# Transposing the third group's attention weights on VectorE, and scattering the merge statistics earlier

## The chip, the cores and the metric

The kernel runs on one core of one Trainium2 chip. The metric is the device time of one execution in microseconds (us). A core has TensorE (PE in the profile, with its weight loads as PEld), VectorE (DVE), ScalarE (ACT), GpSimd (POOL) and SyncE (SP), each with a queue of its own; DMAs are issued from the queues of SP, POOL and ACT.

## The reference

Two decoder layers on 512 tokens of 1024 channels: a mixer, then a SwiGLU FFN with 2816 hidden channels, with an RMSNorm ahead of each and one at the end. The change lies in the first layer's mixer, a mixture of three dilated causal attentions with ALiBi, and in the last step of the first FFN.

```python
ATTN_PAIRS = ((128, 1), (512, 4), (2048, 16))        # (window, dilation) of the three groups, 8 heads of 128 each
...
# group g: query t attends to keys t - j*dil, j = 0..window/dil
s = jnp.einsum('bnqhd,bnkhd->bnhqk', qb, kb) * (D ** -0.5) + bias
p = jnp.exp(s - m); den = jnp.sum(p, axis=-1, keepdims=True)
o = jnp.einsum('bnhqk,bnkhd->bnqhd', p / den, vb)
lse = (m + jnp.log(den))[..., 0]
...
wts = jax.nn.softmax(jnp.stack(lses, axis=0), axis=0)  # over the three groups
o = jnp.sum(wts[..., None] * o, axis=0)
return o.astype(h.dtype) @ w_out
```

So the three groups of one head are one softmax over all their keys: each group contributes a maximum and a sum for each query, and these are merged.

## The kernel before

**Numbers.** Every large product is made in fp32 precision from three fp32r matmuls: an operand is split into a high and a low part (`split`, L77 on ACT and L78 on DVE), and hi x hi, hi x lo and lo x hi are added up in PSUM. Weights arrive by DMA in a ring of raw tiles and are split into a ring of five `whi`/`wlo` pairs, some products ahead of their use (`pump`).

**Products.** Plain products (`Product.add`, L254 to L257) run over 512 columns. From the second head on, two 128-column weight blocks at a time go through `seven`, which makes a 2x2 block product with seven half-size ones (L371 to L373, 12 matmuls of 256 columns each, about 1.44 us) and adds on DVE (L412, L418/L420, L425, L426). It holds four PSUM banks, `p1`, `p26`, `p45` and `p73`, of the eight in the ring `ps()`; a new bank is one that was taken eight allocations before. `values12` (L483 to L485) is the same thing for the values of groups 2 and 3. Between the products, `behind(i)` calls other work that is due there: a dictionary `after` maps the place to functions, and `between(h, g)` writes it for head h's three q/k pairs (g = 0, 1, 2). The tile framework then orders each engine's instructions from that program.

**Token order.** Tokens are stored by residue mod 4 (`r`), so that each residue's 128 tokens (`i`) are one block for groups 2 (dilation 4) and 3 (dilation 16). Group 1 needs them by blocks of 128 neighbours: `by_block` and `in_a_row` are the views that change from one order to the other. At the end of the first FFN `unfold` (L879) puts all tokens in natural order for the pooling layer.

**A head's attention**, one head behind the projections:

- `scores0` and `scores12` make the scores of group 1 (`s0`) and of groups 2 and 3 (`s12`, 128 queries x 4 residues x 2 groups x 128 keys), their maxima on DVE and the exponentials with their sums on ACT (L577, L601). Maxima and sums are kept in `st`: `st[:, 0]` for both orders of queries, a column for each block or residue.
- `merge` brings group 1's statistics to the order of groups 2 and 3 and the other way round. For this it spreads each statistic over four columns, of which `place` leaves one (partition mod 4) non-zero (`far`, L614), multiplies by `swap` on PE (L618; ones where two partitions lie in the same group of four), and picks out and adds up (L621, L624). From both it makes the factors `co`, and scales `s0` on DVE (L633) and `s12` on ACT (L636).
- `turn0` and `turn12` transpose the weights on PE, 128x128 at a time with `ident` (L645, L656), and ACT copies them out of PSUM (L646, L657). `turn_values` (L540) does so for group 1's values.
- `output` multiplies values and transposed weights (L669 to L672, L678).

`far` lies in the buffer of `b12`, the bias tile of `scores12`. A list `mark` holds the last DVE subtraction of each `seven` or `values12`, and `merge` issues `far` behind the latest of them.

Of the kernel before, what the change touches and what calls it, by code (L numbers as in the profile page):

```python
# [2 lines left out]

# [12 lines left out]
P = 128  # L16
S = 512
# [31 lines left out]
def trunk(ctx: ExitStack, tc: tile.TileContext, xT, norms, w_first, w_qk, w_qkp, w_v0, w_v0p, w_v12, w_out, w_pair, w_down, w_pin, w_pgrp,  # L49
# [304 lines left out]

        return t.rearrange("p (a c) -> p a c", a=2)


    mark = []

    def by_block(t, a=slice(0, 2)):  # L360

        return t.rearrange("p (b i r) -> p r i b", b=NT, r=NT)[:, 2 * a.start:2 * a.stop]
# [17 lines left out]
    def seven(T, one, two, scratch, after={}, blocks=False):  # L380


        unit, = units.popleft()
        into, left, right = by_block if blocks else in_place, slice(0, 1), slice(1, 2)

        def again(v):
            return v.unsqueeze(1).to_broadcast([P, 2, H2])

        p1, p26, p45, p73 = ps(), ps(), ps(), ps()

        def behind(i):
# [12 lines left out]
        w = part(unit, "s")  # L404
        mult(p45[:, H2:], w, 0, T, "1")
        behind(2)
        mult(p73[:, :H2], w, 1, T, "3")
        w.done()
        behind(3)
        w = part(unit, "m")  # L410
        mult(p26[:, H2:], w, 0, T, "2")
        nc.vector.tensor_add(into(one), p26, again(first[:, :H2]))  # L412
        behind(4)
        mult(p73[:, H2:], w, 1, T, "22")
        w.done()
        if blocks:
            for a in (left, right):
                nc.vector.tensor_add(in_place(sums, a), in_place(p73, a), into(one, right))  # L418
        else:
            nc.vector.tensor_add(sums, p73, again(one[:, H2:]))  # L420
        behind(5)
        w = part(unit, "l")
        mult(p45[:, :H2], w, 0, T, "4")
        w.done()
        nc.vector.tensor_sub(into(two), p45, again(sums[:, :H2]))  # L425
        mark.append(nc.vector.tensor_sub(into(one, right), sums[:, H2:], p45[:, H2:]))  # L426
        behind(6)

    def normed(layer, k, row):
# [21 lines left out]
    with tc.tile_pool(name="opool", bufs=1) as opool:  # L451
        early = opool.tile([P, HEADS, S], F32R, tag="o", name="early")
        with tc.tile_pool(name="apool", bufs=1) as apool:
# [15 lines left out]
            def values12(after={}):  # L469


                t = apool.tile([P, NT, 4 * P], F32, name="v12")
                unit = units.popleft()

                def product(name, half, key):
                    p = ps()
                    for a in range(2):
                        for k in range(K2):
                            wh, wl = (v[:, half * S + k % 2 * H2:half * S + (k % 2 + 1) * H2]
                                      for v in part(unit[k // 2], name).t)  # L480
# [47 lines left out]
                mark.append(nc.vector.tensor_sub(quarter(0, 1), both(m4), both(u3)))  # L528
                behind(6)
                return t  # L530

# [49 lines left out]
            def scores12(h):  # L581
# [19 lines left out]
                    nc.scalar.activation(v, v, AF.Exp, bias=nm[:, 1, r:r + 1], accum_out=st[:, 0, 1, 1, r:r + 1])  # L601
                A[h]["s12"] = s12

            def merge(h):


                st, s0, s12 = A[h]["st"], A[h]["s0"], A[h]["s12"]
                mx = apool.tile([P, 2, NT], F32, name="mx")
                ex = apool.tile([P, 2, 2, NT], F32, name="ex")
                dd = apool.tile([P, 2, 2, NT], F32, name="dd")  # L610
                co = apool.tile([P, 2, NT], F32, name="co")
                far = apool.tile([P, 4 * NT, NT], F32, tag="b12", name="far")
                with tc.issue_after(mark[-1].ins) if mark else nullcontext():
                    nc.vector.tensor_mul(far, st[:, 0].rearrange("p a s b -> p (a s b)").unsqueeze(2).to_broadcast(  # L614
                        [P, 4 * NT, NT]), place[:, None].to_broadcast([P, 4 * NT, NT]))
                p = ps()
                for a in range(2):
                    nc.tensor.matmul(p[:, a * 32:(a + 1) * 32], swap,  # L618
                                     far[:, (1 - a) * 8:(2 - a) * 8].rearrange("p s r -> p (s r)"), start=True, stop=True)

                nc.vector.tensor_mul(far.rearrange("p (q r) b -> p q r b", r=NT),  # L621
                                     p[:, :64].rearrange("p (q b r) -> p q r b", b=NT, r=NT),
# [26 lines left out]
            def turn12(h):  # L649

                s12 = A[h]["s12"]
                t12 = apool.tile([P, NT, 2, P], F32, name="t12")
                for half in range(2):
                    p = ps()
                    for a in range(4):
                        nc.tensor.transpose(blk(p, a), s12[:, 2 * half + a // 2, a % 2, :], ident)  # L656
                    nc.scalar.copy(t12[:, 2 * half:2 * half + 2].rearrange("p a g k -> p (a g k)"), p)  # L657
                A[h]["t12"] = t12

            def output(h):  # L660
# [15 lines left out]
                for r in range(NT):  # L676
                    for g in (1, 2):
                        nc.tensor.matmul(blk(po, r), blk(QKV[h // 2, 12, 2][:, r, :], h % 2 * 2 + g - 1),  # L678
                                         t12[:, r, g - 1, :],
                                         start=g == 1, stop=g == 2)  # L680
                nc.vector.tensor_add(o0, o0, po)

# [81 lines left out]
            def between(h, g):  # L764

                if g == 0:
                    return {2: [later(merge, h - 1)], 4: [later(turn_values, h - 1)] if h > 1 else []} if h % 2 else {
                        1: [later(output, h - 2)], 2: [later(merge, h - 1)]}
                if g == (2 if h == 1 else 1):
                    return {0: [later(turn0, h - 1)], 2: [later(turn12, h - 1)], 4: [later(scores0, h)]}  # L770
# [17 lines left out]
                prepare(2 + c)  # L788
            scores12(0)
            turn_values(0)  # L790
            for h in range(1, HEADS):
                for g in range(3):
                    if h == 1 and g < NSOLO:
# [17 lines left out]
                        nc.gpsimd.dma_start(X[k], xT[:, k, :])  # L811
                if h % 2 == 0:
                    VT[:] = [apool.tile([P, S], F32, tag=tag, name="vt") for tag in ("row", "o0")]
                    seven(T, *VT, scratch, {0: [later(scores12, h)]}, True)
                elif h < HEADS - 1:
                    QKV[h // 2, 12, 2] = values12({0: [later(scores12, h)]})
                else:
                    QKV[h // 2, 12, 2] = values12({0: [later(scores12, h)], 1: [later(halve, 0), later(halve, 1)],
                                                   2: [later(halve, 2), later(halve, 3)], 3: [later(merge, h)],
                                                   4: [later(halve, 4), later(halve, 5)]})  # L820
            for k in range(KC):
                give(("h", k))
# [29 lines left out]
    with tc.tile_pool(name="fpool", bufs=2) as fpool:  # L852
# [19 lines left out]
        def unfold(m, p):  # L872
# [3 lines left out]
                new = t[:, 0]  # L876
            else:
                new = x_tile(m - 1)
            nc.vector.tensor_add(new.rearrange("p (b i r) -> p r i b", r=NT, b=NT), *(  # L879
                t.rearrange("p (r i b) -> p r i b", r=NT, b=NT) for t in (X[m], p)))  # L880
            X[m] = new

        def ffn(layer, nxt, lead, row):
# [281 lines left out]
```

## Time and profile before

| | |
|---|---|
| runs of the kernel | 1268.6, 1269.49 and 1269.86 us, median 1269.49 |
| profiled execution | 1268.85 us, span from first to last instruction 1267.0 us |
| granted TensorE clock over the span | 0.998 |
| PE busy | 1252.6 us, 8310 instructions |
| DVE busy | 919.1 us, 1383 instructions |
| ACT busy | 566.7 us, 879 instructions |
| attention, first to last head | from the start to about 463 us |
| first FFN | about 510 to 858 us |

A row of the timeline gives start and length in us, engine, line, operation, tiles written and read (buffer numbers left out), shape, how many were merged into the row, and in brackets how long the engine had been idle and what ended that. A row of the groups gives the number of instructions, their joint busy time in us, the mean length of one in ns, and the idle time ahead of them. A row of the waits gives who waited for whom, the total in us, how often, and the longest. PE's records overlap, so the time that a PE instruction takes on its engine is the distance to the next start. An fp32 matmul that isn't split is two records; a transpose is one.

### The profile page before, as it was taken

How to read it: one execution, taken by the hardware profiler on the slowest of the kernel's cores; microseconds unless marked ns; L12 is line 12 of the kernel's file. 1: busy time of each engine (PE TensorE's matmuls, PEld its weight loads, DVE VectorE, ACT ScalarE, POOL GpSimd, SP SyncE). 2: the span in 40 equal slices, each digit the busy share in tenths (PEclk: the TensorE clock that was granted, in tenths of full speed). 3: DMA queues.
4: the chain of work that ended last, by engine and by line, in shares of the span. 5: the costliest groups of instructions: out<-in, count | busy, mean ns of one | idle time of the engine just before them, and what ended most of it. 6: DMA issues, size and time to landing. Idle time of an engine off the chain costs nothing.

```text
span 1267.0 us, 20887 instructions
## 1 busy us (share of the span) xinstructions
PE 1252.6 (99%) x8310; PEld 1154.3 (91%) x8310; DVE 919.1 (73%) x1383; ACT 566.7 (45%) x879; POOL 127.0 (10%) x121
## 2 busy tenths in 40 slices
PE   9999999999999999999999999999999999999997
PEld 7889999999999988889989999888788988999987
DVE  6987788878778845778636887558977853788643
ACT  6445554545445543444424554343444532455331
POOL 2011111211111000001001110000300000111000
PEclk9999999999999999999999999999999999999999
DMA  8336566655756433247457774334124745677322
GB/s 290 105 93 166 132 156 146 159 141 144 180 139 152 138 136 115 67 96 178 131 140 166 182 186 126 99 130 132 38 78 107 173 131 138 171 183 172 93 69 67
DMA packets 67330, 172.45 MB, mean 136 GB/s; under 512 B 6928, under 2 KB 9120, under 8 KB 67232
## 3 DMA queue, kind: packets, MB, share of 16 engines
q1 hardware_dynamic: 48816, 135.97, 34.3%
q0 software_dynamic: 17264, 34.09, 16.1%
q8 instruction: 65, 1.06, 0.3%
q10 hardware_dynamic: 1152, 1.05, 0.2%
q14 instruction: 33, 0.27, 0.1%
HBM read 168.99 MB, written 2.10 MB: 135 GB/s over the span
## 4 chain that ended last, share of the span: by engine, by line
PE 74%; issue 12%; DVE 9%; DMA 2%; ACT 1%; POOL 1%; DVEq 0%; POOLq 0%
PE ps L372 12%; PE ps L371 12%; PE ps L373 12%; PE ps L255 8%; PE ps L254 8%; PE ps L257 8%; DMA raw<-w_pair 2%; PE ps L483 2%; PE ps L484 2%; PE ps L485 2%; DVE wlo L78 2%; PE ps L678 1%; PE ps L590 1%; DVE raw L434 1%; POOL rcol L323 1%
## 5 line engine op out<-in xcount | busy, mean ns | idle before, releaser
L77 ACT ACTIVATE whi<-raw 128x1024 fp32r<-128x1024 f32 (+2 forms) x297 | 295.3, 1000 | 438.4 <-PE ps L255 196.5
L78 DVE TENSOR_TENSOR wlo<-raw,whi 128x1024 fp32r<-128x1024 f32 (+2 forms) x297 | 340.4, 1150 | 150.2 <-ACT whi L77 149.1
L254 PE MATMUL ps<-a,whi 128*128 128x512 f32 (+1 forms) x374 | 141.0, 377 | 0.0
L255 PE MATMUL ps<-a,whi 128*128 128x512 f32 (+1 forms) x374 | 140.9, 377 | 0.0
L257 PE MATMUL ps<-a,wlo 128*128 128x512 f32 (+1 forms) x374 | 140.8, 377 | 0.0
L371 PE MATMUL ps<-tt,whi 128*128 128x256 f32 x384 | 108.7, 283 | 0.0
L372 PE MATMUL ps<-tt,whi 128*128 128x256 f32 x384 | 108.7, 283 | 0.0
L373 PE MATMUL ps<-tt,wlo 128*128 128x256 f32 x384 | 108.7, 283 | 0.0
L137 POOL DMA_DIRECT2D raw<-w_pair x32 | 38.7, 1210 | 446.2 <-DMA raw<-w_pair 158.8
L257 PEld LDWEIGHTS ps<-a,wlo 128*128 128x128 f32 x374 | 70.4, 188 | 13.0
L254 PEld LDWEIGHTS ps<-a,whi 128*128 128x128 f32 x374 | 70.4, 188 | 12.8
L255 PEld LDWEIGHTS ps<-a,whi 128*128 128x128 f32 x374 | 70.4, 188 | 12.7
L371 PEld LDWEIGHTS ps<-tt,whi 128*128 128x128 f32 x384 | 73.7, 192 | 0.0
L372 PEld LDWEIGHTS ps<-tt,whi 128*128 128x128 f32 x384 | 73.7, 192 | 0.0
L373 PEld LDWEIGHTS ps<-tt,wlo 128*128 128x128 f32 x384 | 73.7, 192 | 0.0
L372 PE MATMUL ps<-tb,whi 128*128 128x256 f32 x256 | 72.6, 284 | 0.9 <-DVE tb L78 0.9
L371 PE MATMUL ps<-h,whi 128*128 128x256 f32 x252 | 72.7, 289 | 0.0
L373 PE MATMUL ps<-tb,wlo 128*128 128x256 f32 x256 | 72.4, 283 | 0.0
L371 PE MATMUL ps<-tb,whi 128*128 128x256 f32 x256 | 72.4, 283 | 0.0
L373 PE MATMUL ps<-h,wlo 128*128 128x256 f32 x252 | 71.3, 283 | 0.0
L372 PE MATMUL ps<-h,whi 128*128 128x256 f32 x252 | 71.3, 283 | 0.0
L254 PE MATMUL ps<-h,whi 128*128 128x512 f32 x160 | 62.7, 392 | 0.0
(280 smaller groups left out, 3420.3 us busy)
## 6 DMA issues: line engine op xcount, KB each, us to landing
raw<-w_pair SPq DMA_DIRECT2D x76, 512.0 KB, 4.5
raw<-w_qkp SPq DMA_DIRECT2D x36, 512.0 KB, 4.5
raw<-w_pair POOLq DMA_DIRECT2D x32, 512.0 KB, 7.3
raw<-w_down SPq DMA_DIRECT2D x32, 384.0 KB, 3.1
raw<-w_down SPq DMA_DIRECT2D x32, 320.0 KB, 2.9
raw<-w_v SPq DMA_DIRECT2D x18, 512.0 KB, 4.1
raw<-w_qkp POOLq DMA_DIRECT2D x18, 512.0 KB, 7.2
rawhalf<-w_pair SPq DMA_DIRECT2D x32, 256.0 KB, 3.5
```

Source lines behind the costliest of these rows:

```text
L77: nc.scalar.activation(hi, v, AF.Copy)
L78: nc.vector.tensor_tensor(lo, v, hi.bitcast(F32), op=OP.subtract)
L137: nc.gpsimd.dma_start(self.b.t.rearrange("p (a c) -> p a c", a=2), self.src[:, None, 3 * S:].to_broadcast([P, 2, S]), accum_op=OP.add)
L254: nc.tensor.matmul(self.p[:, cols], w[0][:, s], mh[:, cols], start=self.done == 0, stop=False)
L255: nc.tensor.matmul(self.p[:, cols], w[0][:, s], ml[:, cols], start=False, stop=False)
L257: nc.tensor.matmul(self.p[:, cols], w[1][:, s], mh[:, cols], start=False, stop=self.done == self.n)
L371: nc.tensor.matmul(dst, w.t[0][:, c], th, start=k == 0, stop=False)
L372: nc.tensor.matmul(dst, w.t[0][:, c], tl, start=False, stop=False)
L373: nc.tensor.matmul(dst, w.t[1][:, c], th, start=False, stop=k == K2 - 1)
L483: nc.tensor.matmul(o, mh, wh, start=k == 0, stop=False)
L484: nc.tensor.matmul(o, mh, wl, start=False, stop=False)
L485: nc.tensor.matmul(o, ml, wh, start=False, stop=k == K2 - 1)
```

## The change

**Transposes.** Within each residue the tokens are put in another order (`turned`): the 128 tokens of a residue mod 4 are now four runs of 32, one for each residue mod 16. In group 3 a query attends only to keys of its own residue mod 16, so its 128x128 weights are zero outside the four 32x32 blocks on the diagonal. `turn12` now transposes group 2's four blocks on PE as before, and group 3's with one `nc.vector.transpose` from SBUF to SBUF, which transposes each 32x32 block in place. `t12` is laid out by group first. Masks and the input's order are prepared to match on the host.

**Merge.** A new function `scatter` makes `far` with the two halves of the statistics exchanged, so that one matmul of 64 columns replaces two of 32. It is called in the value stage of the head itself and no longer in `merge` during the next head's first q/k pair, and the list `mark` is gone. For odd heads `merge` and `turn_values` are called one product earlier (at 1 and 3 in place of 2 and 4).

**Unfold.** The new order can't be undone by one view of four dimensions, so the add that ends the first FFN is made in four parts of 128 columns, with both inputs strided and the output contiguous.

```diff
             def merge(h):
-                far = apool.tile([P, 4 * NT, NT], F32, tag="b12", name="far")
-                with tc.issue_after(mark[-1].ins) if mark else nullcontext():
-                    nc.vector.tensor_mul(far, st[:, 0].rearrange("p a s b -> p (a s b)").unsqueeze(2).to_broadcast(
-                        [P, 4 * NT, NT]), place[:, None].to_broadcast([P, 4 * NT, NT]))
                 p = ps()
-                for a in range(2):
-                    nc.tensor.matmul(p[:, a * 32:(a + 1) * 32], swap,
-                                     far[:, (1 - a) * 8:(2 - a) * 8].rearrange("p s r -> p (s r)"), start=True, stop=True)
+                nc.tensor.matmul(p[:, :64], swap, far.rearrange("p s r -> p (s r)"), start=True, stop=True)
...
+            def scatter(h):
+                far = apool.tile([P, 2, 2 * NT, NT], F32, tag="b12", name="far")
+                nc.vector.tensor_mul(far, A[h]["st"][:, 0, ::-1].rearrange("p a s b -> p a (s b)").unsqueeze(3)
+                                     .to_broadcast([P, 2, 2 * NT, NT]), place[:, None, None].to_broadcast([P, 2, 2 * NT, NT]))
+                A[h]["far"] = far.rearrange("p a s r -> p (a s) r")
...
             def turn12(h):
                 s12 = A[h]["s12"]
-                t12 = apool.tile([P, NT, 2, P], F32, name="t12")
-                for half in range(2):
-                    p = ps()
-                    for a in range(4):
-                        nc.tensor.transpose(blk(p, a), s12[:, 2 * half + a // 2, a % 2, :], ident)
-                    nc.scalar.copy(t12[:, 2 * half:2 * half + 2].rearrange("p a g k -> p (a g k)"), p)
+                t12 = apool.tile([P, 2, NT, P], F32, name="t12")
+                p = ps()
+                for r in range(NT):
+                    nc.tensor.transpose(blk(p, r), s12[:, r, 0, :], ident)
+                nc.scalar.copy(t12[:, 0].rearrange("p r k -> p (r k)"), p)
+                nc.vector.transpose(t12[:, 1], s12[:, :, 1, :])
...
-                    return {2: [later(merge, h - 1)], 4: [later(turn_values, h - 1)] if h > 1 else []} if h % 2 else {
+                    return {1: [later(merge, h - 1)], 3: [later(turn_values, h - 1)] if h > 1 else []} if h % 2 else {
                         1: [later(output, h - 2)], 2: [later(merge, h - 1)]}
...
+            scatter(0)
...
-                    seven(T, *VT, scratch, {0: [later(scores12, h)]}, True)
+                    seven(T, *VT, scratch, {0: [later(scores12, h)], 4: [later(scatter, h)]}, True)
...
-                    QKV[h // 2, 12, 2] = values12({0: [later(scores12, h)]})
+                    QKV[h // 2, 12, 2] = values12({0: [later(scores12, h)], 4: [later(scatter, h)]})
...
         def unfold(m, p):
-            nc.vector.tensor_add(new.rearrange("p (b i r) -> p r i b", r=NT, b=NT), *(
-                t.rearrange("p (r i b) -> p r i b", r=NT, b=NT) for t in (X[m], p)))
+            for b in range(NT):
+                nc.vector.tensor_add(new[:, b * P:(b + 1) * P], *(
+                    t.rearrange("p (r j i b) -> p b i j r", r=NT, j=NT, b=NT)[:, b] for t in (X[m], p)))
```

In the last head `scatter` and `merge` both stand in the value stage, at 2 and 3.

How the rows move is shown at head 3's first q/k pair, where head 2 is merged. A number behind a name is that of the buffer; lines of the new kernel are a few lower than the old ones (L620 was L621, L412 is L409). On PE, the second product of `seven` (before `ps_1794`, now `ps_1784`), the third (`ps_1795`, now `ps_1785`) and the exchange; before:

```order
L371 MATMUL ps_1795<-tx_590,whi_1631 128x256
L372 MATMUL ps_1795<-tx_591,whi_1631 128x256
L373 MATMUL ps_1795<-tx_590,wlo_1632 128x256
L371 MATMUL ps_1794<-t_387,whi_1703 128x256
L618 MATMUL ps_1852<-far_1850,const_90 128x32 x2
L371 MATMUL ps_1796<-t_390,whi_1631 128x256
```

And now:

```order
L368 MATMUL ps_1784<-h_587,whi_1589 128x256
L369 MATMUL ps_1784<-h_587,whi_1589 128x256
L370 MATMUL ps_1784<-h_587,wlo_1590 128x256
L618 MATMUL ps_1824<-far_1747,const_90 128x64
L368 MATMUL ps_1785<-t_387,whi_1619 128x256
L369 MATMUL ps_1785<-t_387,whi_1619 128x256
```

The exchange stood behind the third product and one matmul of the fifth; it now stands right behind the second, 13 matmuls earlier, and is one matmul.

On DVE at the same place (`vt` are head 2's values, `raw`, `halflo` and `wlo` the weights of later products), before:

```order
L426 TENSOR_TENSOR vt_1649<-sums_1668,ps_1653 128x2x32x4
L150 TENSOR_TENSOR raw_1594<-raw_1594,raw_1595 128x512
L78 TENSOR_TENSOR halflo_1843<-rawhalf_1596,halfhi_1842 128x512
L151 TENSOR_TENSOR raw_1594<-raw_1594 128x512
L614 TENSOR_TENSOR far_1850<-st_1459,place_457 128x64
L621 TENSOR_TENSOR far_1850<-ps_1852,place_457 128x64
```

And now, from five rows earlier on:

```order
L409 TENSOR_TENSOR vt_1637<-ps_1640,first_1655 128x4x32x4
L606 TENSOR_TENSOR far_1747<-st_1447,place_457 128x64
L78 TENSOR_TENSOR wlo_1731<-raw_1582,whi_1730 128x1024
L415 TENSOR_TENSOR sums_1656<-ps_1642,vt_1637 128x256 x2
L78 TENSOR_TENSOR wlo_1764<-raw_1583,whi_1763 128x1024
L422 TENSOR_TENSOR vt_1638<-ps_1641,sums_1656 128x4x32x4
L423 TENSOR_TENSOR vt_1637<-sums_1656,ps_1641 128x2x32x4
L150 TENSOR_TENSOR raw_1582<-raw_1582,raw_1583 128x512
L78 TENSOR_TENSOR halflo_1856<-rawhalf_1584,halfhi_1855 128x512
L151 TENSOR_TENSOR raw_1582<-raw_1582 128x512
L620 TENSOR_TENSOR far_1747<-ps_1824,place_457 128x64
```

`far` moved from between L151 and the pick-out to right behind the first part of `vt`.

Later in the same pair DVE does the transpose; now:

```order
L422 TENSOR_TENSOR qk01_1782<-ps_1785,sums_1800 128x4x32x4
L423 TENSOR_TENSOR qk00_1781<-sums_1800,ps_1785 128x2x32x4
L78 TENSOR_TENSOR halflo_2004<-rawhalf_1725,halfhi_2003 128x512
L657 STREAM_TRANSPOSE t12_2007<-s12_1658 128x512
L78 TENSOR_TENSOR wlo_1988<-raw_1723,whi_1987 128x1024
L78 TENSOR_TENSOR wlo_2035<-raw_1871,whi_2034 128x1024
```

The transpose is the only row that came in there; before, the split of the `wlo` that follows came right behind `halflo`.

More of the change, by code (lines that the diff above doesn't have):

```diff
@@ L1 @@
 from collections import deque
-from contextlib import ExitStack, nullcontext
+from contextlib import ExitStack
 import concourse.bass as bass
@@ L355, in both @@
         return t.rearrange("p (a c) -> p a c", a=2)
-    mark = []
     def by_block(t, a=slice(0, 2)):
@@ L425, in seven @@
         nc.vector.tensor_sub(into(two), p45, again(sums[:, :H2]))
-        mark.append(nc.vector.tensor_sub(into(one, right), sums[:, H2:], p45[:, H2:]))
+        nc.vector.tensor_sub(into(one, right), sums[:, H2:], p45[:, H2:])
         behind(6)
@@ L527, in values12 @@
                 done("l")
-                mark.append(nc.vector.tensor_sub(quarter(0, 1), both(m4), both(u3)))
+                nc.vector.tensor_sub(quarter(0, 1), both(m4), both(u3))
                 behind(6)
@@ L602, in scores12 @@
                 A[h]["s12"] = s12
+            def scatter(h):
[3 more added lines that the diff above has]
+                A[h]["far"] = far.rearrange("p a s r -> p (a s) r")
             def merge(h):
-                st, s0, s12 = A[h]["st"], A[h]["s0"], A[h]["s12"]
+                st, s0, s12, far = (A[h][name] for name in ("st", "s0", "s12", "far"))
                 mx = apool.tile([P, 2, NT], F32, name="mx")
@@ L678, in output @@
                         nc.tensor.matmul(blk(po, r), blk(QKV[h // 2, 12, 2][:, r, :], h % 2 * 2 + g - 1),
-                                         t12[:, r, g - 1, :],
+                                         t12[:, g - 1, r, :],
                                          start=g == 1, stop=g == 2)
@@ L813, in trunk @@
                     VT[:] = [apool.tile([P, S], F32, tag=tag, name="vt") for tag in ("row", "o0")]
-                    seven(T, *VT, scratch, {0: [later(scores12, h)]}, True)
+                    seven(T, *VT, scratch, {0: [later(scores12, h)], 4: [later(scatter, h)]}, True)
                 elif h < HEADS - 1:
-                    QKV[h // 2, 12, 2] = values12({0: [later(scores12, h)]})
+                    QKV[h // 2, 12, 2] = values12({0: [later(scores12, h)], 4: [later(scatter, h)]})
                 else:
                     QKV[h // 2, 12, 2] = values12({0: [later(scores12, h)], 1: [later(halve, 0), later(halve, 1)],
-                                                   2: [later(halve, 2), later(halve, 3)], 3: [later(merge, h)],
+                                                   2: [later(scatter, h), later(halve, 2), later(halve, 3)],
+                                                   3: [later(merge, h)],
                                                    4: [later(halve, 4), later(halve, 5)]})
@@ L1132 @@
     past = np.where(dd <= 0, dd + P, FAR)
-    c = (NI * np.arange(NT)[None, :] + np.arange(NI)[:, None]).reshape(-1)
+    turned = np.arange(NI).reshape(NI // NT, NT).T.reshape(-1)
+    j = (NT * turned[:, None] + np.arange(NT)[None, :]).reshape(-1)
+    near, past = near[j][:, j], past[j][:, j]
+    c = (NI * np.arange(NT)[None, :] + turned[:, None]).reshape(-1)
     d4 = dd[c][:, c]
     arrays = {
-        "xT": v["x"].reshape(NT, NI, NT, KC, P).transpose(4, 3, 2, 1, 0).reshape(P, KC, S),
+        "xT": v["x"].reshape(NT, NI, NT, KC, P)[:, turned].transpose(4, 3, 2, 1, 0).reshape(P, KC, S),
         "norms": vec.reshape(NORMS, KC, P).transpose(2, 0, 1),
```

## The prediction

> **What bounds the kernel now.** I read the page's engine totals first, then the sums over stretches of time, then the chain of waits and the list of waits.
>
> ```profile
> PE 1252.6 (99%) x8310; PEld 1154.3 (91%) x8310; DVE 919.1 (73%) x1383; ACT 566.7 (45%) x879; POOL 127.0 (10%) x121
> ...
> PE 74%; issue 12%; DVE 9%; DMA 2%; ACT 1%; POOL 1%; DVEq 0%; POOLq 0%
> ...
> 122.00:177.00 55.00, 54.23 (x454) 53.90 (x453) 42.82 (x72) 27.03 (x49) 10.61 (x11) 1.00 0.56 140
> 177.00:232.00 55.00, 55.00 (x461) 54.84 (x460) 45.22 (x69) 28.26 (x50) 6.80 (x7) 1.00 0.67 161
> ...
> ACT whi L77 <- PE ps L255: 196.5, 71, 8.0
> ACT whi L77 <- PE ps L372: 136.8, 98, 3.4
> ...
> PE ps L618 <- DVE far L614: 2.3, 3, 0.8
> ```
>
> TensorE (PE) is busy 99% of the span, and PE work is 74% of the chain that ended last. The two windows are one head pair of the attention (columns: length, then PE, weight loads, DVE, ACT and POOL busy, granted clock): PE is full at a granted clock of 1.00, while DVE has about 10 us free in 55. ACT waits for PE to give weight buffers back (196.5 and 136.8 us), so the weights run ahead of PE and not behind it. In the attention, then, a PE instruction taken out shortens the run by its issue time, and work put on DVE costs nothing until some PE instruction waits for it. The one such wait in the heads' stages is the last row: the exchange matmul at L618 waits for DVE's `far` in three heads.
>
> **The change, part by part.**
>
> *Transposes.* `turn12` has 8 PE transposes per head, and keeps 4.
>
> ```profile
> 90.61 1.04 PE L656 MATMUL ps<-ident,s 128*128 128x128 f32 x8
> 91.48 0.38 PE L564 MATMUL ps<-qk,qk 128*128 128x256 f32 x1
> ...
> L656 PE MATMUL ps<-ident,s 128*128 128x128 f32 x64 | 8.3, 273 | 0.0
> ```
>
> Eight of them start at 90.61 and the next instruction starts at 91.48: 0.87 us, 0.109 each. A record is 273 ns long, but records overlap, so the spacing is what counts. 4 x 8 heads x 0.109 = 3.5 us off PE, all of it on the path. The Trainium skill, "TensorE: Matmul & The Clock Gate", Part 4: PE-mode transpose, gives about 275 ns for a transpose inside a kernel; the trace's record length agrees with that and its spacing does not, and by the page's figure this term would be 8.8 us in place of 3.5.
>
> *Exchange.* Two matmuls of 32 columns become one of 64. Each fp32 matmul is two records, so 4 become 2.
>
> ```profile
> 232.54 0.53 PE L618 MATMUL ps<-far,const 128*128 128x32 f32 x4
> 232.91 0.36 PE L371 MATMUL ps<-t,whi 128*128 128x256 f32 x1
> ...
> 458.66 0.39 PE L671 MATMUL ps<-t,v 128*128 128x128 f32 x2
> 458.88 0.39 PE L672 MATMUL ps<-t,v 128*128 128x128 f32 x2
> ```
>
> Four passes of 32 columns take 0.37 where nothing waits; two passes of 128 columns take 0.22, so a pass costs about 0.11 whether 32 or 128 columns stream, and one of 64 lies between. Two passes saved: 0.22 x 8 = 1.8 us.
>
> *The scatter moves into the value stage.* This is the wait on L618.
>
> ```profile
> 171.60 0.28 PE L371 MATMUL ps<-t,whi 128*128 128x256 f32 x1
> 172.64 0.60 PE L618 MATMUL ps<-far,const 128*128 128x32 f32 x4 [0.77 <-DVE far L614]
> 173.08 0.36 PE L371 MATMUL ps<-t,whi 128*128 128x256 f32 x1
> ...
> 164.53 0.19 ACT L601 ACTIVATION_READ_ACCUMULATOR s<-s,nm 128x1 f32 x1
> 164.60 1.13 DVE L412 TENSOR_TENSOR vt<-ps,first 128x512 f32<-128x512 f32 x1 [2.00 <-PE ps L373]
> ...
> 212.86 0.19 ACT L601 ACTIVATION_READ_ACCUMULATOR s<-s,nm 128x1 f32 x1
> 214.03 1.23 DVE L78 TENSOR_TENSOR wlo<-raw,whi 128x1024 fp32r<-128x1024 f32 x1 [1.45 <-ACT whi L77]
> ```
>
> From 171.60 to 173.08 is 1.48 us. Without the wait it would be one matmul (0.12) and the exchange (0.37), so the stall with its refill is 0.99, in heads 3, 5 and 7: 3.0 us. In the new order `far` is made right behind L412 `vt` (heads 2, 4, 6), after the last statistic was out at 164.72, some 4 us before PE comes to the exchange. In heads 1, 3 and 5 it stands ahead of the weight split at 214.03; its statistic is out at 213.05, and that split waits for ACT until 214.03 in any case, so a wait of `far` there costs nothing. The exchange itself stands 13 matmuls earlier.
>
> *What is late next.* With PE earlier, the next thing DVE holds up is a PSUM bank: the first matmul of the fourth product of q/k pair 1 takes the bank that L426 (`qk`) reads last.
>
> ```profile
> 173.28 0.23 DVE L621 TENSOR_TENSOR far<-ps,place 128x64 f32<-128x64 f32 x1 [0.79 <-PE ps L618]
> 175.81 1.23 DVE L78 TENSOR_TENSOR wlo<-raw,whi 128x1024 fp32r<-128x1024 f32 x1 [0.53 <-ACT whi L77]
> ...
> 183.53 0.70 DVE L426 TENSOR_TENSOR qk<-sums,ps 128x256 f32<-128x256 f32 x1
> 185.53 0.36 PE L371 MATMUL ps<-t,whi 128*128 128x256 f32 x1
> ```
>
> L426 ends at 184.23 and PE starts at 185.53: 1.30 us to spare. PE now comes 0.99 + 0.22 + 0.44 = 1.65 earlier. DVE comes earlier by nothing at least and by its two idle times, 1.32, at most. So PE waits between 0 and 0.35 there, three times: 0 to 1.1 us. I take 0.1 each, 0.3, because the 0.79 goes for certain but the split behind it hangs on an ACT pass that cannot start before L151.
>
> *What moves along.* In odd heads `merge` is called one product earlier, and so is `turn_values` (8 PE transposes, 2 ACT copies); no DMA changes its place on SP's or POOL's queue.
>
> ```profile
> 170.00 0.65 DVE L426 TENSOR_TENSOR vt<-sums,ps 128x256 f32<-128x256 f32 x1
> 175.91 1.03 PE L540 MATMUL ps<-ident,vt 128*128 128x128 f32 x8
> ...
> 179.96 1.08 DVE L633 TENSOR_SCALAR s<-s,co 128x256 f32<-128x256 f32 x4
> 181.10 0.93 PE L645 MATMUL ps<-ident,s 128*128 128x128 f32 x7
> ```
>
> L540's input is ready at 170.65, 5.3 us ahead; one product (1.44) and the 1.21 that merge saves leave 2.6. L645 takes s0 0.06 after L633 has scaled it, and comes 1.21 earlier; but DVE now does L633 ahead of one pass of L412 (0.93), L151 (0.6) and half of L418 (0.5), 2.0 us earlier. Neither waits: 0.
>
> *VectorE's transpose, and ACT's copy.* One STREAM_TRANSPOSE of 512 columns per head; no trace row shows one.
>
> ```profile
> L420 DVE TENSOR_TENSOR sums<-ps,gt 128x512 f32<-128x512 f32 x32 | 21.9, 684 | 3.4 <-PE ps L373 3.2
> L597 DVE TENSOR_REDUCE st<-s 128x4 f32<-128x1024 f32 x8 | 9.7, 1218 | 0.2
> ...
> 188.26 1.23 DVE L78 TENSOR_TENSOR wlo<-raw,whi 128x1024 fp32r<-128x1024 f32 x1 [2.39 <-ACT whi L77]
> 244.34 1.22 DVE L78 TENSOR_TENSOR wlo<-raw,whi 128x1024 fp32r<-128x1024 f32 x1 [0.58 <-ACT whi L77]
> ```
>
> Bounds: a pass over 512 columns, 0.68, and one over 1024, 1.22. I take 0.7, since the same 512 go through once. It stands just ahead of these splits, whose idle (2.39 in odd heads, 0.58 and then more in even ones) hides it: 0. If that cover went, it would be 8 x 0.7 = 5.6. Its reader, the output matmul, comes a group of products later. ACT loses a copy per head, off the path: 0. The Trainium skill, "VectorE: DVE Perf Modes", The three transpose paths, has 311 ns for 128 columns of bf16; four times that would be an estimate of 1.24 us, still under the idle, and the sum would not move.
>
> *Unfold.* One add of 512 columns becomes four of 128 with both inputs strided, for eight tiles at the end of the first FFN.
>
> ```profile
> L879 DVE TENSOR_TENSOR x<-x,ps 128x512 f32<-128x512 f32 x7 | 7.8, 1113 | 9.7 <-PE ps L257 9.7
> L418 DVE TENSOR_TENSOR sums<-ps,qk 128x256 f32<-128x256 f32 x12 | 7.2, 619 | 0.0
> L439 DVE TENSOR_TENSOR raw<-raw 128x256 f32<-128x256 f32 x12 | 5.0, 420 | 0.2
> ...
> 816.73 1.11 DVE L879 TENSOR_TENSOR x<-x,ps 128x512 f32<-128x512 f32 x1 [2.03 <-PE ps L257]
> 821.36 0.82 DVE L78 TENSOR_TENSOR wlo<-raw,whi 128x640 fp32r<-128x640 f32 x1 [1.37 <-ACT whi L77]
> 849.39 0.69 DVE L292 TENSOR_TENSOR acc<-acc,sq 128x512 f32<-128x512 f32 x1
> 857.33 0.95 PE L318 MATMUL ps<-ones,acc 128*128 128x1 f32 x8
> ```
>
> 256 columns take 420 ns and 512 take 684, so 128 take about 288: 1.15 for four without any price on the strides. A strided stream adds 200 ns per 256 columns (619 against 420); two streams on 128 columns add 200, so 1.95 for four. Against 1.11 that is +0.04 to +0.84 per tile. DVE idles 2.03 and 1.37 us per tile there, and the last sum is ready 7.2 us before PE reads it: 0. Uncovered, it would be up to 6.7.
>
> *Sum:* 3.5 + 1.8 + 3.0 - 0.3 = 8.0. The profiled execution took 1268.85 (span 1267.0); it lies 0.64 under the median of the runs, 1269.49. From the median: 1261.5; the profiled one would be 1260.9.
>
> **Rivals.**
>
> *The stall only moves.* PE saves its 5.3 us of instructions, but waits as long for the PSUM bank, or for the exchange, as it did. For it: the 1.30 against 1.65 above. Against it: DVE gets at least part of its 1.32 back. 1269.5 - 5.3 = 1264.2.
>
> *VectorE's transpose is slow, and the kernel ends slower.* After it, DVE may lose 2.4 us of idle and some 0.4 that it comes earlier; then each further us delays L426 of the next pair and with it the bank that PE takes. From about 2.8 us a transpose, seven heads pay the excess, and 8.0 / 7 + 2.8 = 3.9 us is where it decides. At 5 us: 7 x 2.2 = 15.4, less 8.0: 1277. Against it: no DVE row of 512 or 1024 columns above is over 1.22.
>
> *PE does not get the time.* If the supply of split weights set the pace, PE would wait at them instead: 1269.5, no change. The waits of ACT on PE speak against it.
>
> *A transpose frees its whole record.* 32 x 0.273 = 8.7 in place of 3.5: 1256.3. The 0.87 for eight speaks against it. This is the rule of the Trainium skill's page on TensorE cited above.
>
> **How the numbers follow.** About 0.2% (2.5 us) is what a measurement of this kernel can tell from no change. The sum as it stands, between 1260 and 1262.8: 0.72; stall moved, 1263 to 1265: 0.14; whole records: 0.04; no change: 0.05; slower: 0.04; the last 0.01 I leave to a gain of another size. So faster 0.91, same 0.05, slower 0.04. I predict 1261.5. The range starts at 1260.0, where no bank wait is left and the runs spread as they do (0.9 below the median); it ends at 1264.8, which takes in the moved stall with its spread.
>
> **What would show it.** PE with 8262 instructions, transposes 32 and exchange records 16; 0.36 us from the start of four transposes to the next matmul; no wait of L618 on `far`; `far` in the value stage with at most half a microsecond of waiting for ACT; STREAM_TRANSPOSE x8 near 0.7 us; a PE wait on L423 `qk` three times, none or up to 0.35; DVE x1415; no new PE wait between 800 and 860. A PE wait for t12, for a weight split or for a bank in every head would prove the sum wrong.

## The result, and the profile after

| | before | after |
|---|---|---|
| median of the runs | 1268.69 us (6 runs, 1267.65 to 1269.86) | 1260.19 us (6 runs, 1259.36 to 1261.30) |
| ratio, 95% interval | | 0.9932, 0.9922 to 0.9942 |
| profiled execution, span | 1268.85 us, 1267.0 us | 1261.29 us, 1259.5 us |

The changed kernel is faster by 8.5 us (by the interval, 7.4 to 9.9); 8.0 were predicted. Two single executions among the runs told of below, one with the transpose made four times over (2498 us, the one that was profiled) and one with the unfold made three times over (3182 us), took about two and two and a half times as long as all others, and the medians and ratios given are without them.

From the page of the new kernel, its engine totals, its chain of what ended last, and two of its groups:

```profile
PE 1247.1 (99%) x8262; PEld 1149.4 (91%) x8262; DVE 927.3 (74%) x1415; ACT 563.6 (45%) x871; POOL 123.0 (10%) x121
...
PE 80%; issue 11%; DVE 6%; DMA 1%; POOL 1%; ACT 1%; SPq 0%; POOLq 0%; DVEq 0%; ACTq 0%
...
L618 PE MATMUL ps<-far,const 128*128 128x64 f32 x16 | 2.7, 246 | 0.0
...
L657 DVE STREAM_TRANSPOSE t<-s 128x512 f32<-128x512 f32 x8 | 5.7, 707 | 0.0
```

PE has the 48 instructions fewer. Its share of the final chain rose from 74 to 80% while DVE's fell from 9 to 6; these shares move by far more than 8.5 us, so they do not size the gain. The exchange has 16 records and no idle time ahead of it. VectorE's transpose takes 707 ns, where 0.7 us was taken.

The timeline of the new kernel around head 2's merge, and where that head's weights are transposed (PE first, then DVE):

```profile
169.70 0.33 PE L618 MATMUL ps<-far,const 128*128 128x64 f32 x2
169.84 0.36 PE L368 MATMUL ps<-t,whi 128*128 128x256 f32 x1
...
183.06 0.60 PE L654 MATMUL ps<-ident,s 128*128 128x128 f32 x4
183.42 0.36 PE L368 MATMUL ps<-t,whi 128*128 128x256 f32 x1
```

```profile
165.10 0.22 DVE L606 TENSOR_TENSOR far<-st,place 128x64 f32<-128x64 f32 x1
...
182.42 0.68 DVE L423 TENSOR_TENSOR qk<-sums,ps 128x256 f32<-128x256 f32 x1
...
183.51 0.73 DVE L657 STREAM_TRANSPOSE t<-s 128x512 f32<-128x512 f32 x1
184.13 1.22 DVE L78 TENSOR_TENSOR wlo<-raw,whi 128x1024 fp32r<-128x1024 f32 x1
186.15 1.22 DVE L78 TENSOR_TENSOR wlo<-raw,whi 128x1024 fp32r<-128x1024 f32 x1 [0.80 <-ACT whi L77]
```

`far` is ready 4.4 us before PE comes to the exchange, which no longer waits. The four transposes give way after 0.36 us, as stated beforehand. L423 has read its bank by 183.10, and PE takes it at 183.42: 0.32 us to spare and no wait.

For the account, take PE in the heads, from one and the same matmul near the start to the first matmul behind the last head. Both kernels were run once more (told below); these rows are of those two executions, the old kernel's first:

```profile
9.61 0.39 PE L254 MATMUL ps<-early,whi 128*128 128x512 f32 x1
...
454.20 0.48 PE L254 MATMUL ps<-oh,whi 128*128 128x512 f32 x1
```

```profile
9.45 0.40 PE L254 MATMUL ps<-early,whi 128*128 128x512 f32 x1
...
445.71 0.48 PE L254 MATMUL ps<-oh,whi 128*128 128x512 f32 x1
```

It is 444.59 us against 436.26, 8.33 less. Laid side by side, instruction by instruction, the two come apart at three kinds of places only: by 0.436 at each of 8 transposes (3.5), by 0.223 at each of 8 exchanges (1.8), and by 1.00 more at the exchanges of heads 3, 5 and 7 (3.0).

### The profile page after: what moved, and what is told of

Read it like the earlier page. It is cut to its first block, busy times and chain, and to the rows that moved or that the text cites. A ratio compares the mean times of both kernels' runs of the same rounds, so it can differ in the third digit from the quotient of the medians.

```text
span 1259.5 us, 20807 instructions
## 1 busy us (share of the span) xinstructions
PE 1247.1 (99%) x8262; PEld 1149.4 (91%) x8262; DVE 927.3 (74%) x1415; ACT 563.6 (45%) x871; POOL 123.0 (10%) x121
## 3 DMA queue, kind: packets, MB, share of 16 engines
q8 instruction: 65, 1.06, 0.3%
## 4 chain that ended last, share of the span: by engine, by line
PE 80%; issue 11%; DVE 6%; DMA 1%; POOL 1%; ACT 1%; SPq 0%; POOLq 0%; DVEq 0%; ACTq 0%
PE ps L369 13%; PE ps L368 13%; PE ps L370 13%; PE ps L254 9%; PE ps L255 9%; PE ps L257 9%; PE ps L481 2%; PE ps L482 2%; PE ps L483 2%; DVE wlo L78 1%; PE ps L678 1%; PE ps L588 1%; DMA raw<-w_pair 1%; DVE n L302 1%; POOL rcol L323 1%
```

## The experiments

Every kernel is timed against the old one on the same chip. Ratios are to the old kernel, with their 95% intervals.

**Each part alone.** First, the scatter into the value stage, with the new places of `merge` and `turn_values`, and without the other parts.

```diff
+            def scatter(h):
...
+                far = apool.tile([P, 4 * NT, NT], F32, tag="b12", name="far")
...
             def merge(h):
...
-                far = apool.tile([P, 4 * NT, NT], F32, tag="b12", name="far")
-                with tc.issue_after(mark[-1].ins) if mark else nullcontext():
...
-                    return {2: [later(merge, h - 1)], 4: [later(turn_values, h - 1)] if h > 1 else []} if h % 2 else {
+                    return {1: [later(merge, h - 1)], 3: [later(turn_values, h - 1)] if h > 1 else []} if h % 2 else {
...
-                    seven(T, *VT, scratch, {0: [later(scores12, h)]}, True)
+                    seven(T, *VT, scratch, {0: [later(scores12, h)], 4: [later(scatter, h)]}, True)
```

> The old kernel with the early scatter alone: `far` made in the value stage, the two exchange matmuls of 32 columns kept, all eight PE transposes per head kept, merge and turn_values of odd heads one product earlier as in the new kernel. Theory (the sum): the stall at the exchange in heads 3, 5 and 7 goes, 3 x 0.99 = 3.0 us, so 1265.7 against 1268.7, and no wait of the exchange on `far` is left. Rival (the stall only moves): PE waits about as long for the bank that qk reads last, or for the exchange, and the gain is 0 to 1 us, 1267.7 to 1268.7.

1265.14 us, 0.9973 (0.9962 to 0.9985): 3.2 us less. Its timeline at head 2's merge:

```profile
165.12 0.22 DVE L608 TENSOR_TENSOR far<-st,place 128x64 f32<-128x64 f32 x1
...
169.72 0.53 PE L622 MATMUL ps<-far,const 128*128 128x32 f32 x4
170.09 0.36 PE L371 MATMUL ps<-t,whi 128*128 128x256 f32 x1
```

The four passes take 0.37 with no wait, and nothing else on PE has become later: the steps at the three merges are 1.06, 0.98 and 1.00. The stall did not move, and the rival with a gain of 0 to 1 us lies outside the interval.

Second, the exchange as one matmul, with `far` still made in `merge`.

```diff
-                for a in range(2):
-                    nc.tensor.matmul(p[:, a * 32:(a + 1) * 32], swap,
-                                     far[:, (1 - a) * 8:(2 - a) * 8].rearrange("p s r -> p (s r)"), start=True, stop=True)
+                nc.tensor.matmul(p[:, :64], swap, far.rearrange("p s r -> p (s r)"), start=True, stop=True)
```

> The old kernel with one exchange matmul of 64 columns in place of two of 32, `far` still made inside merge at its old place. Theory: 8 x 0.22 = 1.8 us less, 1266.9, and the stall of about 1 us in heads 3, 5 and 7 stays as it was. Rival (a pass costs by its columns, so two passes of 64 take as long as four of 32): 0, 1268.7. A second rival: the wait on `far` grows by what PE saves, so that only the five heads without a stall gain, 5 x 0.22 = 1.1, 1267.6.

1267.14 us, 0.9988 (0.9979 to 0.9997): 1.2 us by the medians, 0.4 to 2.7 by the interval, which cannot tell 1.8 from 1.1. The timeline can: a merge without a stall, one with it, and the list of waits.

```profile
122.90 0.33 PE L618 MATMUL ps<-far,const 128*128 128x64 f32 x2
123.04 0.36 PE L371 MATMUL ps<-t,whi 128*128 128x256 f32 x1
...
171.69 0.28 PE L371 MATMUL ps<-t,whi 128*128 128x256 f32 x1
172.74 0.41 PE L618 MATMUL ps<-far,const 128*128 128x64 f32 x2 [0.77 <-DVE far L614]
172.95 0.36 PE L371 MATMUL ps<-t,whi 128*128 128x256 f32 x1
...
PE ps L618 <- DVE far L614: 2.3, 3, 0.8
```

Two passes of 64 columns take 0.14 where four of 32 took 0.37, and the stalled place takes 1.26 where it took 1.48: 0.22 to 0.23 less in both. The wait is as long as before; it did not take up the gain. Over the eight merges PE's steps add up to 1.8 us.

Third, the token order, VectorE's transpose and the four-part unfold, with the old merge.

```diff
-                for half in range(2):
+                for r in range(NT):
+                    nc.tensor.transpose(blk(p, r), s12[:, r, 0, :], ident)
...
+                nc.vector.transpose(t12[:, 1], s12[:, :, 1, :])
```

> The old kernel with the token order, VectorE's transpose of the third group and the four-part unfold; the merge is the old one. Theory: 32 transposes at 0.109 us of PE, 3.5 us less, 1265.2; the stall in heads 3, 5 and 7 stays. Rival (a transpose frees its whole record, 273 ns): 8.7 less, 1260.0. Rival (the added DVE work is not hidden): at most 3.5 - 5.6 = 2.1 us slower than the kernel before, 1270.8, with PE waiting for DVE in the heads or at the end of the first FFN.

1264.89 us, 0.9972 (0.9960 to 0.9983): 3.5 us less. This kernel has 32 PE transposes fewer, 0.109 each. A gain of 8.7 would be a ratio of 0.9931, outside the interval. The stall was there as before (2.3 us in three heads). The three parts alone give 3.2, 1.2 and 3.5 by the medians, 7.9 in all, and 3.05, 1.8 and 3.5 by PE's steps: they add up.

**Does the earlier place of merge matter?** The new kernel with `merge` and `turn_values` of odd heads back where they stood.

```diff
-                    return {1: [later(merge, h - 1)], 3: [later(turn_values, h - 1)] if h > 1 else []} if h % 2 else {
+                    return {2: [later(merge, h - 1)], 4: [later(turn_values, h - 1)] if h > 1 else []} if h % 2 else {
```

> The new kernel with merge and turn_values of the odd heads put back to their old places (2 and 4 in place of 1 and 3). Theory: the early `far` alone takes the stall away, and the place of merge costs nothing: 1260.2 as the new kernel, within 0.5 us. Rival (the place matters): the scaling of s0 comes one product, 1.4 us, later, turn0 takes s0 with only about 2 us to spare, and PE waits for it or for the bank that qk reads last: up to 1 us in each of three or four heads, 1261 to 1264.

1259.85 us, 0.9931 (0.9919 to 0.9944): the same as the new kernel. The early `far` alone takes the stall away.

**How much DVE work do the heads hide?** VectorE's transpose is made four, seven and ten times over, on the same tile; the edit for four:

```diff
-                nc.vector.transpose(t12[:, 1], s12[:, :, 1, :])
+                for again in range(4):
+                    nc.vector.transpose(t12[:, 1], s12[:, :, 1, :])
```

> The new kernel with VectorE's transpose made four times over (the same tile, the same result), about 2.8 us of DVE per head in place of 0.7. The prediction put the cover at about 2.8 us per head (2.4 us of DVE idle in that stretch and 0.4 of earlier start). Theory: just hidden, 1260.2 to 1262. Rival (the cover is smaller, since PE now takes qk's bank with 0.32 us to spare): seven heads pay 1 to 2 us each, 1267 to 1274.

> The new kernel with VectorE's transpose made seven times over, about 4.9 us of DVE per head. Theory (a cover of 2.8 us, then each further us delays qk and the bank that PE takes): 7 x 2.1 to 2.2 = 15 us slower than the new kernel, 1275. Rival (DVE's idle time in the other stages of a head takes the delay in, so that it is not on PE's path): 1260 to 1263. Rival (no cover at all): 8 x 4.2 = 34 us slower, 1294.

Four times: 1260.5 us, 0.9937 (0.9924 to 0.9951), not to be told from the new kernel. Seven times: 1263.35 us, 0.9960 (0.9948 to 0.9973), 3 us above it and far from 1275 or 1294. The trace for four comes from a second run, and ten times shows what limits in the end:

> The kernel with VectorE's transpose made four times over, once more, for a trace of it. Theory (what counts is where DVE next hands something to PE, not the bank after the transpose): no PE wait on a bank or on qk in any head, or under 0.1 us in heads 3, 5 and 7 at the scores of groups 2 and 3; 1260 to 1261.5. Rival (a cover of 2.4 us behind the transpose): PE waits 0.4 us or more for the bank in seven heads, 1263.

> The new kernel with VectorE's transpose made ten times over: about 7 us per head, 6.35 more than in the new kernel, where DVE is busy 45.1 us of 54.4 in a mean head. Theory (the idle time of DVE up to the next thing that PE takes from it counts; with seven transposes that was the scores' qk in heads 3, 5 and 7, by 0.56 to 1.15 us): the 2.1 us more delay qk by up to 2.1 in these heads and begin to show in the even ones, 6 to 9 us more than with seven, 1269 to 1273. Rival (the prediction's cover of 2.8 us per head, each us beyond it lost in seven heads): 7 x 4.25 = 30 us above the new kernel, 1290. Rival (DVE's free 9.3 us per head take in all of it): as with seven, 1263.4.

The second run of four, a single execution, took 1261.45 us. Ten times: 1267.46 us, 0.9990 (0.9980 to 1.0000), 7.3 above the new kernel and 1.5 below the lower end of the theory's range; the even heads lost 0.1 to 0.3 us each. The groups and waits of seven, then of ten:

```profile
L658 DVE STREAM_TRANSPOSE t<-s 128x512 f32<-128x512 f32 x56 | 39.5, 705 | 0.9
...
PE ps L588 <- DVE qk L422: 1.8, 3, 1.0
```

```profile
L658 DVE STREAM_TRANSPOSE t<-s 128x512 f32<-128x512 f32 x80 | 56.2, 703 | 1.1
...
PE ps L588 <- DVE qk L422: 4.6, 3, 1.7
...
PE ps L679 <- DVE t L658: 0.4, 1, 0.4
```

With four, no such wait is in the list. The main place is the same in both: the scores of groups 2 and 3 (L588) in heads 3, 5 and 7, which wait for the last q/k pair. With ten, the output of the last head (L679) also waits for the transpose itself. The rows of head 3, with four, seven and ten:

```profile
200.77 0.69 DVE L422 TENSOR_TENSOR qk<-ps,sums 128x512 f32<-128x512 f32 x1
...
202.72 1.95 PE L588 MATMUL ps<-qk,qk 128*128 128x128 f32 x16
```

```profile
203.19 0.68 DVE L422 TENSOR_TENSOR qk<-ps,sums 128x512 f32<-128x512 f32 x1
...
203.14 0.39 PE L588 MATMUL ps<-qk,qk 128*128 128x128 f32 x2
203.93 1.83 PE L588 MATMUL ps<-qk,qk 128*128 128x128 f32 x14 [0.40 <-DVE qk L422]
```

```profile
204.34 0.68 DVE L422 TENSOR_TENSOR qk<-ps,sums 128x512 f32<-128x512 f32 x1
...
203.22 0.39 PE L588 MATMUL ps<-qk,qk 128*128 128x128 f32 x2
205.08 0.60 PE L588 MATMUL ps<-qk,qk 128*128 128x128 f32 x3 [1.47 <-DVE qk L422]
```

PE needs L422's result at its third instruction here, 0.22 behind the first. With four transposes it is there 1.48 us too soon (201.46 against 202.94), as with one (1.49 in the first trace): in this head DVE's idle time took in the first 2.1 us whole. The next 2.1 us use up the 1.48 and make PE late by 0.57 (203.93 against 203.36); with ten it is late by 1.64 (205.08 against 203.44), so DVE's idle time took in about half of the last 2.1. Head 7 has less room: with four, 0.39 us were left to spare there. In no kernel of the series did PE wait for the bank behind the transpose. DVE's busy time in a stretch of two heads, 120 to 229 us, in the new kernel, with four, seven and ten:

```profile
120.00:229.00 109.00, 109.00 (x913) 108.68 (x911) 90.89 (x141) 55.25 (x98) 16.47 (x17) 1.00 0.62 157
```

```profile
120.00:229.00 109.00, 109.00 (x912) 108.68 (x912) 94.36 (x148) 54.38 (x97) 16.63 (x17) 1.00 0.64 155
```

```profile
120.00:229.00 109.00, 108.60 (x907) 108.09 (x906) 97.38 (x153) 54.84 (x97) 15.76 (x17) 1.00 0.63 155
```

```profile
120.00:229.00 109.00, 107.52 (x894) 106.81 (x894) 99.86 (x158) 53.39 (x97) 15.81 (x17) 1.00 0.62 150
```

DVE is the third busy time of a row: 90.9, 94.4, 97.4, 99.9 of 109. PE (the first) starts to lose with 11.6 us of DVE still free, so it is not the sum of DVE's idle time that sets the limit: the first to come late is one delivery in each odd head.

**Is the unfold hidden?** The four adds of each tile three times over.

```diff
-            for b in range(NT):
+            for b in [b for again in range(3) for b in range(NT)]:
```

> The new kernel with the four strided adds of each unfolded tile made three times over (12 adds, the same result): about 2.6 to 3 us more of DVE per tile, 8 tiles. Theory: DVE idles 3.4 us per tile there and the last sum is ready 7 us before PE reads it, so nothing changes: 1260.2, within 0.5. Rival (these adds lie on the path, since they hold PSUM banks and the weight splits behind them): 8 x 2.5 = 20 us slower, 1280.

1261.0 us, 0.9940 (0.9927 to 0.9954). The groups of the new kernel, then of this one:

```profile
L882 DVE TENSOR_TENSOR x<-x,ps 128x128 f32<-128x128 f32 x28 | 9.2, 382 | 9.2 <-PE ps L257 9.2
```

```profile
L882 DVE TENSOR_TENSOR x<-x,ps 128x128 f32<-128x128 f32 x84 | 25.6, 377 | 0.0
```

16 us more of DVE, and between 570 and 890 us its trace has no PE wait that the new kernel's has not. The median is 0.8 above the new kernel's with intervals that overlap. What its trace loses lies elsewhere: at waits told of next and in the last section, and 0.34 us at the scores of head 7, where DVE was held up by this row ahead of the last q/k pair:

```profile
407.26 1.23 DVE L78 TENSOR_TENSOR wlo<-raw,whi 128x1024 fp32r<-128x1024 f32 x1 [1.86 <-ACT whi L77]
```

The new kernel's two traces have 0.23 us of idle time or none there. So with a single transpose, too, the last q/k pair can reach the scores (L588) late, when a weight comes late.

**Two waits that the change does not touch.** In the first two traces PE also differed by 0.6 us at a split of `tb` in the first FFN (in the old kernel alone) and by 1.0 us at the first weights (in the new one alone). Both kernels once more, unchanged:

> The old kernel once more. The new kernel's trace does not show the wait of 0.62 us for a split of `tb` at the first FFN's first seven-product step, and it shows a wait of 1.07 us for the first weights that the old one does not. Theory (both hang on when a DMA lands, and change from run to run): the `tb` wait comes out another length, anywhere from 0 to 0.7, with a start that differs by up to 1 us. Rival (they belong to the kernels): 0.6 at `tb` again, and no wait above 0.5 for the first weights.

> The new kernel once more. Theory (DMA arrival): a start without the wait of 1.07 us for the first weights, or with another length, and a `tb` wait at the first FFN anywhere from 0 to 0.7. Rival (they belong to the new kernel): 1.07 and none again. In the heads the steps of PE against the old kernel are the same as in the first trace to within 0.05 us: 0.44 at each turn12, 0.22 at each exchange, about 1.0 more in heads 3, 5 and 7.

1268.06 and 1259.06 us. The old kernel's row at `tb` in the first trace, then in the second:

```profile
566.55 0.39 PE L372 MATMUL ps<-tb,whi 128*128 128x256 f32 x1 [0.47 <-DVE tb L78]
```

```profile
565.89 0.28 PE L372 MATMUL ps<-tb,whi 128*128 128x256 f32 x1
```

The wait is gone in the old kernel itself, and the new kernel's start is 1 us shorter in its second trace. Over all the traces of this study PE's idle time at this place lies between nothing and 0.62 us (the unfold three times over), in versions of both kernels. So neither belongs to the change; that a DMA's landing sets them fits, and was not tried by itself.

**A version that might be better.** In the new kernel the second fp32r matmul behind fp32 work starts about 0.08 us late. Here such work is put together: merge right behind output, turn0 beside turn12.

```diff
-                        1: [later(output, h - 2)], 2: [later(merge, h - 1)]}
+                        1: [later(output, h - 2), later(merge, h - 1)]}
...
-                    return {0: [later(turn0, h - 1)], 2: [later(turn12, h - 1)], 4: [later(scores0, h)]}
+                    return {2: [later(turn0, h - 1), later(turn12, h - 1)], 4: [later(scores0, h)]}
```

> The new kernel with fp32 work put together: merge of the even heads right behind output (at 1 in place of 2), turn0 and turn12 at one place (both at 2). Theory: each change from fp32 to fp32r matmuls costs PE some 0.08 us (the second fp32r matmul behind it starts that much later than elsewhere), 3 + 6 or so of them are saved: 0.7 us less, 1259.5. Rival (no such cost; or the places matter for DVE): 1260.2 or, if the exchange or turn0 comes before its input is ready, slower by 0.5 to 1 us a head, up to 1266.

1259.61 us, 0.9931 (0.9918 to 0.9945): no difference. The exchange behind output in this kernel:

```profile
120.97 0.33 PE L618 MATMUL ps<-far,const 128*128 128x64 f32 x2
121.12 0.36 PE L368 MATMUL ps<-t,whi 128*128 128x256 f32 x1
121.32 0.28 PE L369 MATMUL ps<-t,whi 128*128 128x256 f32 x1
```

The late start is the other half of an early one. Two fp32 passes give way after 0.15 us, which is less than twice the 0.109 of a pass inside fp32 work, and the second matmul behind them comes at 0.20 in place of 0.12. Together that is about 0.23, with or without fp32 work ahead: a switch costs nothing to speak of, and there is none to save. By PE's steps this kernel saves 8.15 us in the heads, the new one 8.30. No version here beats the new kernel.

## Why the prediction was right

**Transposes.** 3.5 us, by PE's steps and by the kernel that has this part alone. The spacing of 0.109 was the right price. The rule of the Trainium skill, "TensorE: Matmul & The Clock Gate", Part 4: PE-mode transpose (about 275 ns inside a kernel), agrees with the length of a record, 273 ns, but not with what a transpose costs PE behind another.

**Exchange.** 0.223 at each of eight, 1.8 us, as taken.

**Stall.** 3.0 us taken, 3.0 measured (1.01, 1.00 and 1.01 beyond the exchange's own 0.22). PE has one more wait in the heads that the prediction does not name, 0.2 us once in the first (L540 in the old kernel); it is alike in both kernels. For heads 1, 3 and 5 `far` was to cost nothing beside a wait that DVE has in any case, and that is what the trace shows:

```profile
210.97 0.23 DVE L606 TENSOR_TENSOR far<-st,place 128x64 f32<-128x64 f32 x1 [0.50 <-ACT s L599]
211.92 1.23 DVE L78 TENSOR_TENSOR wlo<-raw,whi 128x1024 fp32r<-128x1024 f32 x1 [0.72 <-ACT whi L77]
```

**The bank wait is the term that was wrong:** 0.3 us taken, none measured. PE came to the fourth product at 183.42 in place of 185.53, and 0.45 of these 2.11 it had gained ahead of the merge, so 1.66 (1.65 had been worked out). DVE's L423 ended at 183.10 in place of 184.23; less the same 0.45, it came 0.68 earlier, of an upper bound of 1.32. 1.30 - 1.66 + 0.68 is the 0.32 to spare seen above. The 0.79 that had been called certain did not come whole, but with it the working itself left 0.44 to spare and no wait: the 0.1 per head was caution that no row backed.

**What was costed at nothing** came out at nothing: VectorE's transpose, the unfold (its four adds took 1.28 us in a row, inside the range of 1.15 to 1.95), the moved merge and `turn_values`.

**The rivals.** A stall that only moves is excluded by the scatter alone; a run without gain and whole records by the times. The rival that ends slower named a mechanism that none of these kernels showed: beyond 2.8 us a transpose, seven heads were to lose the excess at a bank, 1277 us at 5 us. At 4.9 us the kernel took 1263.35, three heads lost 0.57 to 1.15 us each, and at another place. The cover was looked for up to the first idle stretch of DVE behind the transpose; it reaches on to the next result that PE takes from DVE with little to spare. The estimate of 1.24 us for 512 columns, four times the 311 ns that the Trainium skill, "VectorE: DVE Perf Modes", The three transpose paths, has for 128 columns of bf16, was too high; 707 ns were measured.

The gain came out 0.5 us above the sum (8.5 against 8.0), of which 0.3 is that bank wait. The rest is less than the interval tells; a step of 0.45 us that goes with the change is in the last section. The time itself, 1260.19 against 1261.5, lies only 0.2 above the lower end of the range. Of these 1.3 us 0.8 are the old kernel's own: its median was 1269.49 in the three runs that the forecast started from and 1268.69 in the six beside the new kernel. The gain is the better measure of the forecast.

## What to carry to other kernels

On an engine that is full, price an instruction by the distance between starts and not by the length of its record, and a wait by the stretch that it lengthens. To move work to another engine, follow that engine's order from there to the next result that the full engine needs, and count all idle time up to it and what that result has to spare: in head 3 here, idle time hid 2.1 us beyond the one transpose and the spare another 1.5, 3.6 us in all. Before an unexpected step is put down to a change, run both kernels again and see which steps come back.

## What the hardware showed that was not expected

**A pass of 64 columns costs no more than one of 32.** Four passes of 32 columns take 0.37 us to the next start, and 0.45 with the late start of the second matmul behind them; two of 64 take 0.14 to 0.15, and 0.23 with it. That is about 0.11 a pass in both.

**A wait on POOL goes with DVE's count of instructions.** At the norm near 910 us PE gained 0.45 us, in the new kernel and in every version with 1415 instructions on DVE (five traces), and in none with another count (eight). The old kernel, then the new one:

```profile
917.22 0.16 DVE L321 TENSOR_SCALAR var<-ps 128x4 f32<-128x4 f32 x1 [0.16 <-PE ps L318]
917.33 1.23 DVE L78 TENSOR_TENSOR wlo<-raw,whi 128x1024 fp32r<-128x1024 f32 x1
917.46 1.97 POOL L323 TENSOR_TENSOR rcol<-var,nhalf 128x4 f32<-128x4 f32 x1 [2.16 <-DVE var L321]
```

```profile
909.24 0.16 DVE L321 TENSOR_SCALAR var<-ps 128x4 f32<-128x4 f32 x1
909.48 1.02 POOL L323 TENSOR_TENSOR rcol<-var,nhalf 128x4 f32<-128x4 f32 x1 [2.15 <-DVE var L321]
909.69 1.23 DVE L78 TENSOR_TENSOR wlo<-raw,whi 128x1024 fp32r<-128x1024 f32 x1 [0.29 <-issue]
```

Where DVE's split starts first, POOL's small operation takes 1.97 us; where DVE is held up by 0.29 for nothing that the profile shows, POOL starts first and takes 1.02. The Trainium skill, "SBUF — State Buffer", Who interferes with whom, has DVE and GpSimd take turns at one shared pair of ports; these rows agree with that for POOL, while the split took 1.23 us either way. What holds DVE up at that place is open; that it goes with the count would fit the position in its stream of instructions, which is not shown.
